# Attention's 256- and 128-column prompt products split into three products of high and low halves, with the scores one step later

## The chip, the cores and the metric

The kernel runs on one core of a Trainium2 chip. The metric is the device time of one execution in microseconds (us), the median of a few runs. TensorE (PE) multiplies; its weight loads are shown apart as PEld. VectorE (DVE) and ScalarE (ACT) do the elementwise work, GpSimd (POOL) a few small things and some transfers, and SyncE (SP) issues nearly all transfers, one after the other in one queue. Each engine takes its instructions strictly in the order written for it.

## The reference

One layer of a streaming encoder for two groups that share the weights: 256 prompt frames and 64 sample frames, 2048 features each. What matters here is the attention, eight heads of 128 features. For the prompt it is, per block of 128 queries and per head:

```python
z = jnp.einsum('bqhd,bkhd->bhqk', q_blk, k) * (SB_HEAD_DIM ** -0.5)
mask = k_pos[None, :] < q_pos[:, None]
log_beta = jax.nn.log_sigmoid(z)
log_stay = jnp.where(mask, jax.nn.log_sigmoid(-z), 0.0)
log_rest = lax.cumsum(log_stay, axis=3, reverse=True) - log_stay
w = jnp.where(mask, jnp.exp(log_beta + log_rest), 0.0)
o = jnp.einsum('bhqk,bkhd->bqhd', w, v)
```

Around it stand one wide input projection (q, k, v, a gating branch, merge gates), two branch projections, an output projection and a gated feed-forward net of 5632 features, with RMS norms between. All is float32.

## The kernel before

**Tiling.** Features lie on the 128 partitions, the 320 frames (256 prompt, 64 sample) on the free axis. A large projection is computed as blocks of 128 output features. Every float32 operand is split into a high half, rounded to the float32r format, and a low half, the rest. A product then is three float32r products: high x high, high x low, low x high (`product`, lines 83 to 85), each with 128 x 128 weights and 320 columns.

**Weight steps.** `block` walks over its input features in steps of eight blocks. A step loads 512 KB of weights (`raw`, line 70, three buffers), makes the high half `wh` on ACT (line 75) and the low half `wl` on DVE (line 76), four buffers each, and issues 24 products on PE. After each step `tick()` runs what was registered with `at` for that tick. I number the steps from 1, starting behind the opening phase (lines 183 to 280), which works off the first two heads in an order of its own. Step n's `raw` needs the buffer that the `wl` of step n-3 has read; step n's `wh` needs the buffer that PE has read in step n-4.

**Attention.** Heads go in four pairs, 0 to 3. For a pair `attend` registers, counted from the tick at which its q, k and v are there: `att_scores` (2 later), the transpose `att_turn` of v (6), the join of v (8), the load of cached v rows `att_rows` (11), `att_turn` of the weights w (12), their join (14) and `att_out` (16). `att_scores` has the score products on PE (lines 361, 362, 364), masking on DVE (368 to 371), three activations on ACT (376 to 378), suffix sums on DVE (386), a difference on DVE (389), exponentials on ACT (390 to 393) and a split of each float32 into two 16-bit planes (`apart`, 334). `att_turn` transposes the planes by a DMA from SP's queue (339), `att_join` puts them together on DVE (`together`, 344). `att_out` multiplies w with v (421), and ACT and DVE split the result into halves (117 and 118, 435 and 436). Score and output products are plain float32 here; the profile shows two PE rows for each.

**Order.** The kernel's text gives the work its sequence, but the framework lays out the order of each engine (and which of the rotating buffers is used) by a list scheduler of its own, within the data's dependencies; only the opening phase and what is marked with `keep_in_program_order` is fixed. So the order on DVE, ACT and SP has to be read from the built program, as below. PSUM has three `acc` buffers for the projections, four `aux` for attention, and a single `aux1`, which `att_out` and the norm `rms` (line 151) share. The tag `B` has 32 buffers for split activations of 320 columns.

Of the kernel before, what the change touches and what calls it, by code (L numbers as in the profile page):

```python
# [8 lines left out]
F32 = mybir.dt.float32  # L9
F32R = mybir.dt.float32r  # L10
AF = mybir.ActivationFunctionType
ALU = mybir.AluOpType

P = 128
TP = 256
# [18 lines left out]
def stream_step(ctx: ExitStack, tc: tile.TileContext, xT, w_in, w_a, w_b, w_out, w_gu, w_down,  # L34
                gains, ws_t, bs, ck_t, cv, y_t, k_t, v_t, sv_t):
    nc = tc.nc
# [21 lines left out]
    def at(tick, fn, *a):  # L58
        assert tick > state["tick"], (tick, state["tick"])
        later.setdefault(tick, []).append((fn, a))  # L60
# [38 lines left out]
    def slot(tag):  # L99
        return big.tile([P, T], F32R, tag=tag, bufs=32, name=tag)  # L100
# [182 lines left out]
    attn = {}  # L283
# [23 lines left out]
    Z, KT = 384, T + PAST  # L307
# [35 lines left out]
    def together(to, src):  # L343
        nc.vector.tensor_copy(to.bitcast(U16).rearrange("p (n w) -> p w n", w=2), src)
# [6 lines left out]
    def att_rows(p):  # L351
        cvt = attn[p]["cv"] = apool.tile([P, 2, 2, P], F32, tag="cv", name="cv")
        tc.keep_in_program_order(nc.sync.dma_start(out=cvt.rearrange("p i h d -> p i (h d)"),
                                                   in_=cv[:, :, 2 * p * P : (2 * p + 2) * P]))

    def att_scores(p):
        s = attn[p]
        q, k = s["q"], s["k"]
        za, zs = (aux(), aux()), aux()
        for j in range(2):  # L360
            nc.tensor.matmul(za[j][:, 0:P], q[:, j, 0:P], k[:, j, 0:P], start=True, stop=True)  # L361
            nc.tensor.matmul(za[j][:, P:Z], q[:, j, P:TP], k[:, j, 0:TP], start=True, stop=True)  # L362
        for j, r in enumerate(ROWS):
            nc.tensor.matmul(zs[r, 0 : KT - TP], q[:, j, TP:T], k[:, j, TP:KT], start=True, stop=True)  # L364
        z = s["z"] = pair("z0"), pair("z1")[:, 0 : Z + TS]
        for j in range(2):
            diag = [t[:, 0:Z].rearrange("p (i t) -> p i t", i=3)[:, 0:3:2, :] for t in (z[j], za[j])]
            nc.vector.tensor_tensor(out=diag[0], in0=diag[1], in1=mdiag.unsqueeze(1).broadcast_to([P, 2, P]), op=ALU.add)
            nc.vector.tensor_copy(z[j][:, P : 2 * P], za[j][:, P : 2 * P])
        nc.vector.tensor_tensor(out=z[1][:, Z:], in0=zs[:, 0:TS], in1=mown, op=ALU.add)  # L370
        nc.vector.tensor_copy(z[0][:, Z:], zs[:, TS : TS + PAST])

        es = []
        for zz in z:
            e = pair("e")[:, : zz.shape[1]]
            nc.scalar.activation(out=e, in_=zz, func=AF.Abs)
            nc.scalar.activation(out=e, in_=e, func=AF.Exp, scale=-1.0)
            nc.scalar.activation(out=e, in_=e, func=AF.Ln, bias=1.0)
            nc.vector.scalar_tensor_tensor(out=e, in0=zz, scalar=0.0, in1=e, op0=ALU.max, op1=ALU.add)
            es.append(e)  # L380


        for j, lo, hi, begin in ((0, 0, P, 0.0), (0, P, Z, 0.0), (1, 0, P, 0.0), (1, P, Z, 0.0),
                                 (1, Z, Z + TS, 0.0), (0, Z, Z + PAST, es[1][:, Z : Z + 1])):
            back = es[j][:, lo:hi][:, ::-1]
            nc.vector.tensor_tensor_scan(out=back, data0=ones[:, 0:1].broadcast_to([P, hi - lo]), data1=back,
                                         initial=begin, op0=ALU.mult, op1=ALU.add)
        for zz, e in zip(z, es):
            nc.vector.tensor_tensor(out=zz, in0=zz, in1=e, op=ALU.subtract)
        nc.scalar.activation(out=z[0], in_=z[0], func=AF.Exp)  # L390
        nc.scalar.activation(out=z[1][:, 0:Z], in_=z[1][:, 0:Z], func=AF.Exp)
        for r in ROWS:
            nc.scalar.activation(out=wown[r, r], in_=z[1][r, Z:], func=AF.Exp)

        y = s["wp"] = planes("wp0", 5 * P), planes("wp1", 4 * P)
        apart(y[0], z[0])
        apart(y[1][:, :, 0:Z], z[1][:, 0:Z])
        apart(y[1][:, :, Z:], wown)
# [7 lines left out]
    def att_join(p, what):  # L406
        s = attn[p]
        t = s[what]
        if what == "vt":
            av = s["av"] = apool.tile([P, 5 * P], F32, tag="av", name="av")  # L410
            together(av, t[0])
        else:
            wt = s["wt"] = apool.tile([P, 9 * P], F32, tag="wt", name="wt")
            together(wt[:, 0 : 5 * P], t[0])
            together(wt[:, 5 * P :], t[1])

    def att_out(p):
        s = attn.pop(p)
        wt, av, cvt = s["wt"], s["av"], s["cv"]
# [6 lines left out]
                lo = Z + i * P + j * TS  # L426
                mm(po[0][:, TP + j * TS : TP + (j + 1) * TS], cvt[:, i, j, :], wt[:, lo : lo + TS], False, i == 1)
        for j in range(2):
            w = wt[:, j * 5 * P : j * 5 * P + Z]
            mm(po[j][:, 0:TP], av[:, 2 * j * P : (2 * j + 1) * P], w[:, 0:TP], True, False)  # L430
            mm(po[j][:, P:TP], av[:, (2 * j + 1) * P : (2 * j + 2) * P], w[:, TP:], False, True)
        aT[2 * p] = split("B", po[0][:, 0:T])
        hi, lo = aT[2 * p + 1] = slot("B"), slot("B")
        for r, src in ((slice(0, TP), po[1][:, 0:TP]), (slice(TP, T), po[0][:, T : T + TS])):
# [24 lines left out]
                head_out(name, first[b][h][:, :T], h)  # L459

    def attend(p, now):
        at(now + 2, att_scores, p)
        at(now + 6, att_turn, p, "vt")
        at(now + 11, att_rows, p)
        at(now + 8, att_join, p, "vt")
        at(now + 12, att_turn, p, "wt")
        at(now + 14, att_join, p, "wt")
        at(now + 16, att_out, p)

    att_new(0)  # L470
    at(state["tick"] + 1, first_out)
# [248 lines left out]
```

## Time and profile before

| | us |
|---|---|
| median of 3 runs | 1709.8 (1708.69 to 1710.63) |
| profiled execution | 1708.48 |
| its span, first to last instruction | 1706.7 |
| PE busy | 1693.9 (99%) |
| DVE busy | 870.2 (51%) |
| ACT busy | 670.0 (39%) |
| POOL busy | 42.2 (2%) |

The granted TensorE clock is 0.997 over the span. Matmuls overlap in the rows, so what one costs in a stream is the distance from its start to the next one's start, not its own duration. Attention's work lies between about 48 and 255 us of the span; the rest is projections.

### The profile page before, as it was taken

The page shows a single profiled execution, that of the slowest core. Times are in us where ns is not written, and L with a number is a line of the kernel's source. Part 1 is how long each engine was busy: PE and PEld are TensorE (multiplying, and loading weights), DVE is VectorE, ACT ScalarE, POOL GpSimd, SP SyncE. Part 2 cuts the span into 40 slices and gives each one's busy share as a digit, 9 for nine tenths or more (in the row PEclk, how much of TensorE's full clock was granted, in tenths as well). Part 3 has the DMA queues.
Part 4 walks back from the last instruction along what each step waited for, and adds up shares of the span by engine and source line. Part 5 has one row for each costly group of instructions (what it writes and reads, how often), then busy time and mean ns, then how long its engine had stood idle before and what let it go on. Part 6 is the DMA issues. An engine that isn't in the chain of part 4 may idle for free.

```text
span 1706.7 us, 27337 instructions
## 1 busy us (share of the span) xinstructions
PE 1693.9 (99%) x11540; PEld 1688.5 (99%) x11540; DVE 870.2 (51%) x1105; ACT 670.0 (39%) x838; POOL 42.2 (2%) x65
## 2 busy tenths in 40 slices
PE   9999999999999999999999999999999999999997
PEld 9999999999999999999999999999999999999997
DVE  7665557544444445555444444444444444444455
ACT  6655555433333333443333332333333333333342
POOL 0000011000000000110000000000000000000000
PEclk9999999999999999999999999999999999999998
DMA  7575566544444445554444444444444444444453
GB/s 254 158 224 172 170 187 166 155 149 149 148 148 150 151 157 168 174 164 148 148 149 149 150 150 153 151 149 149 148 149 149 151 152 152 149 149 148 132 151 113
DMA packets 100299, 268.30 MB, mean 157 GB/s; under 512 B 28976, under 2 KB 35376, under 8 KB 100176
## 3 DMA queue, kind: packets, MB, share of 16 engines
q1 hardware_dynamic: 98672, 263.23, 48.7%
q0 software_dynamic: 1088, 3.02, 0.5%
q8 instruction: 90, 1.47, 0.3%
q10 hardware_dynamic: 416, 0.31, 0.1%
q14 instruction: 33, 0.27, 0.0%
HBM read 256.03 MB, written 5.51 MB: 153 GB/s over the span
## 4 chain that ended last, share of the span: by engine, by line
issue 54%; PE 44%; DVE 0%; DMA 0%; ACT 0%; POOL 0%; POOLq 0%; ACTq 0%; DVEq 0%
PE acc L83 14%; PE acc L84 13%; PE acc L85 13%; PE aux L219 2%; PE acc L219 1%; PE aux L421 1%; DVE h L659 0%; DMA raw<-w_in 0%; PE aux L530 0%; PE aux L362 0%; PE aux L364 0%; PE aux L361 0%; POOL sq_h L175 0%; PE aux L155 0%; PE aux L657 0%
## 5 line engine op out<-in xcount | busy, mean ns | idle before, releaser
L75 ACT CAST wh<-raw 128x1024 fp32r<-128x1024 f32 x468 | 484.2, 1036 | 962.8 <-PE acc L84 748.9
L76 DVE TENSOR_TENSOR wl<-raw,wh 128x1024 fp32r<-128x1024 f32 x468 | 564.6, 1207 | 477.9 <-ACT wh L75 477.1
L83 PE MATMUL acc<-A,wh 128*128 128x320 f32 x2464 | 762.9, 310 | 0.0
L84 PE MATMUL acc<-A,wh 128*128 128x320 f32 x2464 | 761.4, 309 | 0.0
L85 PE MATMUL acc<-A,wl 128*128 128x320 f32 x2464 | 761.4, 309 | 0.0
L83 PEld LDWEIGHTS acc<-A,wh 128*128 128x128 f32 x2464 | 462.6, 188 | 2.1 <-issue 2.0
L84 PEld LDWEIGHTS acc<-A,wh 128*128 128x128 f32 x2464 | 462.6, 188 | 0.2
L85 PEld LDWEIGHTS acc<-A,wl 128*128 128x128 f32 x2464 | 462.6, 188 | 0.0
L85 PE MATMUL acc<-B,wl 128*128 128x320 f32 x960 | 296.6, 309 | 0.0
L83 PE MATMUL acc<-B,wh 128*128 128x320 f32 x960 | 296.6, 309 | 0.0
L84 PE MATMUL acc<-B,wh 128*128 128x320 f32 x960 | 296.6, 309 | 0.0
L83 PEld LDWEIGHTS acc<-B,wh 128*128 128x128 f32 x960 | 180.2, 188 | 0.0
L84 PEld LDWEIGHTS acc<-B,wh 128*128 128x128 f32 x960 | 180.2, 188 | 0.0
L85 PEld LDWEIGHTS acc<-B,wl 128*128 128x128 f32 x960 | 180.2, 188 | 0.0
L83 PE MATMUL acc<-mh,wh 128*128 128x320 f32 x256 | 79.1, 309 | 0.0
L84 PE MATMUL acc<-ml,wh 128*128 128x320 f32 x256 | 79.1, 309 | 0.0
L85 PE MATMUL acc<-mh,wl 128*128 128x320 f32 x256 | 79.1, 309 | 0.0
L619 DVE TENSOR_TENSOR bb<-acc,rh 128x320 f32<-128x320 f32 x44 | 21.6, 492 | 57.8 <-PE acc L85 57.8
L616 DVE TENSOR_TENSOR ev<-acc,rh 128x320 f32<-128x320 f32 x44 | 21.6, 492 | 56.6 <-PE acc L85 56.6
L83 PEld LDWEIGHTS acc<-mh,wh 128*128 128x128 f32 x256 | 48.0, 188 | 0.0
L84 PEld LDWEIGHTS acc<-ml,wh 128*128 128x128 f32 x256 | 48.0, 188 | 0.0
L85 PEld LDWEIGHTS acc<-mh,wl 128*128 128x128 f32 x256 | 48.0, 188 | 0.0
(158 smaller groups left out, 691.9 us busy)
## 6 DMA issues: line engine op xcount, KB each, us to landing
raw<-w_gu SPq DMA_DIRECT2D x176, 512.0 KB, 3.6
raw<-w_in SPq DMA_DIRECT2D x141, 512.0 KB, 3.8
raw<-w_down SPq DMA_DIRECT2D x80, 512.0 KB, 3.5
raw<-w_out SPq DMA_DIRECT2D x32, 512.0 KB, 3.6
raw<-w_a SPq DMA_DIRECT2D x16, 512.0 KB, 3.5
raw<-w_b SPq DMA_DIRECT2D x16, 512.0 KB, 3.5
raw<-w_down SPq DMA_DIRECT2D x16, 256.0 KB, 2.6
xr<-xT SPq DMA_DIRECT2D x16, 160.0 KB, 2.6
```

Of the source, the lines that this page charges most:

```text
L75: nc.scalar.copy(out=wh[:, : n * P], in_=raw[:, : n * P])
L76: nc.vector.tensor_tensor(out=wl[:, : n * P], in0=raw[:, : n * P], in1=wh[:, : n * P].bitcast(F32), op=ALU.subtract)
L83: nc.tensor.matmul(ps[:, :T], a, x[0], start=first, stop=False)
L84: nc.tensor.matmul(ps[:, :T], a, x[1], start=False, stop=False)
L85: nc.tensor.matmul(ps[:, :T], b, x[0], start=False, stop=last)
L219: nc.tensor.matmul(first[b][h][:, :T], w[:, (h * n + j) * P : (h * n + j + 1) * P], xs[c + j][i], start=not last and c + j + i == 0, stop= ...
L421: mm = lambda out, a, b, first, last: nc.tensor.matmul(out, a, b, start=first, stop=last, skip_group_check=True)
L616: nc.vector.tensor_tensor(out=t, in0=pg, in1=got["rh"], op=ALU.mult)
L619: nc.vector.tensor_tensor(out=u, in0=pu, in1=got["rh"], op=ALU.mult)
```

## The change

`parts` splits a tile on the fly: the high half on ACT, the low half on DVE, each into a buffer of tag `B`. The prompt's queries, keys, v rows and weights w are split that way, ten splits per pair (eight of 256 columns, two of 128). Each prompt product of the scores and of the outputs becomes three float32r products. The sample's products (64 columns, and the 320-column product with 64 weight columns) stay as they are. `att_parts` runs one tick ahead of where the scores stood, and `att_scores`, `att_rows`, the turn and join of w and `att_out` come one tick later; the turn and join of v keep their ticks. The diff:

```diff
+    def parts(src):
+
+        n = src.free_size()
+        hi, lo = (slot("B")[:, 0:n] for _ in range(2))
+        view = lambda t: t.rearrange("p (j d) -> p j d", j=src.shape[1]) if len(src.shape) == 3 else t
+        nc.scalar.copy(out=view(hi), in_=src)
+        nc.vector.tensor_tensor(out=view(lo), in0=src, in1=view(hi.bitcast(F32)), op=ALU.subtract)
+        return hi, lo
+
+
+    THREE = ((0, 0), (0, 1), (1, 0))
+
+    def att_parts(p):
+        s = attn[p]
+        s["qp"] = parts(s["q"][:, :, P:TP])
+        s["q0"] = parts(s["q"][:, :, 0:P])
+        s["kp"] = [parts(s["k"][:, j, 0:TP]) for j in range(2)]
+
     def att_scores(p):
         s = attn[p]
-        q, k = s["q"], s["k"]
+        q, k, qp = s["q"], s["k"], s["qp"]
         za, zs = (aux(), aux()), aux()
         for j in range(2):
-            nc.tensor.matmul(za[j][:, 0:P], q[:, j, 0:P], k[:, j, 0:P], start=True, stop=True)
-            nc.tensor.matmul(za[j][:, P:Z], q[:, j, P:TP], k[:, j, 0:TP], start=True, stop=True)
+            for a, b in THREE:
+                nc.tensor.matmul(za[j][:, 0:P], s["q0"][a][:, j * P : (j + 1) * P], s["kp"][j][b][:, 0:P],
+                                 start=a + b == 0, stop=a == 1)
+            for a, b in THREE:
+                nc.tensor.matmul(za[j][:, P:Z], qp[a][:, j * P : (j + 1) * P], s["kp"][j][b], start=a + b == 0, stop=a == 1)
...
         if what == "vt":
             av = s["av"] = apool.tile([P, 5 * P], F32, tag="av", name="av")
             together(av, t[0])
+            s["ap"] = parts(av[:, 0 : 4 * P].rearrange("p (j d) -> p j d", j=2)[:, :, 0:P])
+            s["a1"] = parts(av[:, 0 : 4 * P].rearrange("p (j d) -> p j d", j=2)[:, :, P : 2 * P])
         else:
             wt = s["wt"] = apool.tile([P, 9 * P], F32, tag="wt", name="wt")
             together(wt[:, 0 : 5 * P], t[0])
             together(wt[:, 5 * P :], t[1])
+            s["tp"] = [parts(wt[:, j * 5 * P : j * 5 * P + TP]) for j in range(2)]
+            s["t1"] = [parts(wt[:, j * 5 * P + TP : j * 5 * P + Z]) for j in range(2)]
...
         for j in range(2):
-            w = wt[:, j * 5 * P : j * 5 * P + Z]
-            mm(po[j][:, 0:TP], av[:, 2 * j * P : (2 * j + 1) * P], w[:, 0:TP], True, False)
-            mm(po[j][:, P:TP], av[:, (2 * j + 1) * P : (2 * j + 2) * P], w[:, TP:], False, True)
+            for a, b in THREE:
+                mm(po[j][:, 0:TP], s["ap"][a][:, j * P : (j + 1) * P], s["tp"][j][b], a + b == 0, False)
+            for a, b in THREE:
+                mm(po[j][:, P:TP], s["a1"][a][:, j * P : (j + 1) * P], s["t1"][j][b], False, a == 1)
...
     def attend(p, now):
-        at(now + 2, att_scores, p)
+        at(now + 1, att_parts, p)
+        at(now + 3, att_scores, p)
         at(now + 6, att_turn, p, "vt")
-        at(now + 11, att_rows, p)
+        at(now + 12, att_rows, p)
         at(now + 8, att_join, p, "vt")
-        at(now + 12, att_turn, p, "wt")
-        at(now + 14, att_join, p, "wt")
-        at(now + 16, att_out, p)
+        at(now + 13, att_turn, p, "wt")
+        at(now + 15, att_join, p, "wt")
+        at(now + 17, att_out, p)
```

On PE the scores of pairs 0 to 3 stood ahead of steps 5, 15, 27 and 39, and stand now ahead of steps 6, 16, 28 and 40; `att_out` stood ahead of steps 19, 29, 41 and 53 and stands ahead of 20, 30, 42 and 54. The norm of the gating branch (the product of `sq_v` at line 155, into `aux1`) stood one whole step of 24 products behind the last `att_out`; now four products lie between them.

**Pair 1, the joins of w on DVE.** Names: `wl_n` is a step's low half, `av` and `wt` the joined v and w, `turned` what the transposes brought. Before, the row of `wl_1479` is step 23 and that of `wl_1512` is step 24:

```order
L76 TENSOR_TENSOR wl_1447<-raw_1444,wh_1446 128x1024
L118 TENSOR_TENSOR B_1332<-aux1_1320,B_1331 128x320
L436 TENSOR_TENSOR B_1336<-aux_1321,B_1335 128x256
L436 TENSOR_TENSOR B_1336<-aux1_1320,B_1335 128x64
L344 COPY av_1409<-turned_1341 128x2x640
L76 TENSOR_TENSOR wl_1479<-raw_1476,wh_1478 128x1024
L344 COPY wt_1611<-turned_1539 128x2x640
L344 COPY wt_1611<-turned_1541 128x2x512
L447 TENSOR_TENSOR k_1074<-acc_1348,rx_571 128x320
L76 TENSOR_TENSOR wl_1512<-raw_1509,wh_1511 128x1024
```

Now, from `wl_1567` (step 23) to `wl_1598` (step 24):

```order
L76 TENSOR_TENSOR wl_1567<-raw_1564,wh_1566 128x1024
L118 TENSOR_TENSOR B_1450<-aux1_1430,B_1449 128x320
L344 COPY av_1489<-turned_1392 128x2x640
L462 TENSOR_TENSOR B_1454<-aux_1431,B_1453 128x256
L462 TENSOR_TENSOR B_1454<-aux1_1430,B_1453 128x64
L362 TENSOR_TENSOR B_1492<-av_1489,B_1491 128x256
L362 TENSOR_TENSOR B_1496<-av_1489,B_1495 128x256
L344 COPY wt_1748<-turned_1665 128x2x640
L344 COPY wt_1748<-turned_1667 128x2x512
L473 TENSOR_TENSOR k_1106<-acc_1399,rx_571 128x320
L76 TENSOR_TENSOR wl_1598<-raw_1595,wh_1597 128x1024
```

The low half of step 24 stands behind the joins of w as it did, while the scores that these joins go back to stand one step later; and step 23's has moved ahead of the join of v.

**Pair 3, the join of v on DVE and its turn on SP.** Before, DVE has from the last difference on (`wl_2288`, `wl_2318` and `wl_2357` are steps 43, 44 and 45):

```order
L389 TENSOR_TENSOR z0_2088<-z0_2088,e_2096 128x640
L118 TENSOR_TENSOR B_2200<-aux1_2188,B_2199 128x320
L436 TENSOR_TENSOR B_2204<-aux_2189,B_2203 128x256
L76 TENSOR_TENSOR wl_2288<-raw_2285,wh_2287 128x1024
L436 TENSOR_TENSOR B_2204<-aux1_2188,B_2203 128x64
L76 TENSOR_TENSOR wl_2318<-raw_2315,wh_2317 128x1024
L344 COPY av_2345<-turned_2276 128x2x640
L491 TENSOR_TENSOR ev_2278<-acc_2215,rx_571 128x320
L76 TENSOR_TENSOR wl_2357<-raw_2354,wh_2356 128x1024
```

and now (`wl_2510` is step 44, `wl_2557` step 45; step 43's stands ahead of the whole chain of the scores):

```order
L410 TENSOR_TENSOR z0_2307<-z0_2307,e_2315 128x640
L118 TENSOR_TENSOR B_2429<-aux1_2409,B_2428 128x320
L76 TENSOR_TENSOR wl_2510<-raw_2507,wh_2509 128x1024
L518 TENSOR_TENSOR ev_2470<-acc_2378,rx_571 128x320
L462 TENSOR_TENSOR B_2433<-aux_2410,B_2432 128x256
L462 TENSOR_TENSOR B_2433<-aux1_2409,B_2432 128x64
L344 COPY av_2537<-turned_2468 128x2x640
L76 TENSOR_TENSOR wl_2557<-raw_2554,wh_2556 128x1024
```

The low half of step 45 stays behind the join of v. On SP the turn stood behind the 46th transfer of weights and stands now behind the 47th, whose buffer is free when step 44's low half is done.

**Pair 3, the exponentials on ACT.** `vs` is the first work of the gating branch, a GELU. Before:

```order
L376 ACTIVATE e_2096<-z0_2088 128x640
L376 ACTIVATE e_2101<-z1_2089 128x448
L377 ACTIVATE e_2096<-e_2096 128x640
L377 ACTIVATE e_2101<-e_2101 128x448
L378 ACT_TABLE_LOAD
L378 ACTIVATE e_2096<-e_2096 128x640
L378 ACTIVATE e_2101<-e_2101 128x448
L75 CAST wh_2287<-raw_2285 128x1024
```

and now:

```order
L519 ACT_TABLE_LOAD
L519 ACTIVATE vs_2151<-ev_2236 128x320
L171 ACTIVATE sq_v_2150<-vs_2151 128x320
L75 CAST wh_2479<-raw_2477 128x1024
L397 ACTIVATE e_2315<-z0_2307 128x640
L397 ACTIVATE e_2320<-z1_2308 128x448
L398 ACT_TABLE_LOAD
L398 ACTIVATE e_2315<-e_2315 128x640
L398 ACTIVATE e_2320<-e_2320 128x448
L399 ACT_TABLE_LOAD
L399 ACTIVATE e_2315<-e_2315 128x640
L399 ACTIVATE e_2320<-e_2320 128x448
```

A GELU has come ahead of pair 3's activations, and with it a table load ahead of line 398.

## Prediction

> **What bounds the kernel.** I read the page's busy times first, then the list of waits.
>
> ```profile
> PE 1693.9 (99%) x11540; PEld 1688.5 (99%) x11540; DVE 870.2 (51%) x1105; ACT 670.0 (39%) x838; POOL 42.2 (2%) x65
> PEld acc L83 <- issue: 2.0, 4, 0.5
> ACT wh L75 <- PE acc L84: 748.9, 339, 3.5
> ```
>
> PE is busy for 99% of the span, and the longest wait in front of its weight loads sums to 2.0 us. ACT waits 748.9 us for PE to give a weight buffer back: it runs ahead of PE by the four buffers. So PE's order is the whole time, and an edit costs what it adds to PE's own stream plus what it makes PE wait. The 51% and 39% of the helpers are averages; in the attention part they must be read place by place.
>
> **The products.** The timeline of PE around pair 0's scores:
>
> ```profile
> 62.54 0.31 PE L84 MATMUL acc<-A,wh 128*128 128x320 f32 x1
> 62.69 0.31 PE L85 MATMUL acc<-A,wl 128*128 128x320 f32 x1
> 62.84 0.38 PE L361 MATMUL aux<-k,q 128*128 128x128 f32 x2
> 63.06 0.60 PE L362 MATMUL aux<-k,q 128*128 128x256 f32 x2
> 63.49 0.39 PE L361 MATMUL aux<-k,q 128*128 128x128 f32 x2
> 63.71 0.60 PE L362 MATMUL aux<-k,q 128*128 128x256 f32 x2
> 64.24 0.76 PE L364 MATMUL aux<-k,q 128*64 128x320 f32 x4
> 64.93 0.41 PE L83 MATMUL acc<-A,wh 128*128 128x320 f32 x1
> ```
>
> From start to start a float32r product of 320 columns takes 0.147 (62.54 to 62.69 to 62.84; 24 of them, a step, 3.52). A float32 product is two rows: 0.22 for 128 columns (62.84 to 63.06), 0.43 for 256 (63.06 to 63.49), so one head's two take 0.65. The change turns each into three. No float32r product of 256 or 128 columns is in this trace. At the rate of the 320-column ones they take 0.147 x 256/320 = 0.117 and 0.059. But narrow products meet another limit, seen in pair 0's outputs:
>
> ```profile
> 116.73 1.00 PE L421 MATMUL aux<-wt,cv 128*128 128x64 f32 x8
> 117.57 1.53 PE L421 MATMUL aux<-wt,av 128*128 128x256 f32 x8
> ```
>
> Eight rows of 64 columns need 0.84, or 0.105 each, as long as a row of 128 columns (0.22/2 = 0.11), though they stream half as much: with 128 new weight columns each, a row does not go below about 0.11. I take 0.11 for 128 columns and 0.117 for 256: 3 x 0.227 = 0.68 per head in place of 0.65. There are 16 such heads (four pairs, two heads, scores and outputs): 16 x 0.03 = +0.5 us. Lower end, with no such limit: 3 x (0.059 + 0.117) = 0.53, 16 x -0.12 = -2.0. Upper end, a 128-column product at the whole float32 price: 3 x (0.22 + 0.117) = 1.01, 16 x 0.36 = +5.8. I take the 0.11 because the 64-column rows are nearest: same weights, narrow stream. The Trainium skill, page "TensorE: Matmul & The Clock Gate", section "Back-to-back issue gap", states about 81 ns per product of 128 columns in a stream of weight loads and products. By that figure the term would be an estimated 16 x (3 x (0.081 + 0.117) - 0.65) = -0.9; the rows here show 0.105 to 0.11, for float32.
>
> **The splits.** Ten casts on ACT and ten subtractions on DVE per pair, most of 256 columns:
>
> ```profile
> L209 ACT CAST wh<-raw 128x256 fp32r<-128x256 f32 x2 | 0.8, 398 | 1.2 <-DMA raw<-w_in 1.2
> L210 DVE TENSOR_TENSOR wl<-raw,wh 128x256 fp32r<-128x256 f32 x2 | 0.8, 422 | 1.0 <-ACT wh L209 1.0
> L75 ACT CAST wh<-raw 128x1024 fp32r<-128x1024 f32 x452 | 474.3, 1050 | 947.9 <-PE acc L84 734.0 <-issue 164.7 <-DMA raw<-w_in 42.1
> ```
>
> At most 10 x 0.40 = 4.0 on ACT and 4.2 on DVE per pair. I cost those of q and k at nothing: they run ahead of the scores, when ACT is waiting for a buffer. Those of v and w stand beside the joins, where DVE waits for transposes anyway. If that cover is gone, they add directly to the slips below.
>
> **Who is late next.** PE is fed by `wl`, which DVE makes in order, between attention's work. I compare, in the trace, when a low half ends and when PE needs it (the first L85 of that step). Pair 0, step 9, behind the whole chain of the scores:
>
> ```profile
> 77.92 3.49 DVE L76 TENSOR_TENSOR wl<-raw,wh 128x1024 fp32r<-128x1024 f32 x3
> 79.41 0.31 PE L85 MATMUL acc<-A,wl 128*128 128x320 f32 x1
> ```
>
> The first of the three ends at 77.92 + 1.23 = 79.1, needed at 79.4 (four steps behind 64.93): 0.3 to spare. Here the change moves chain and need together, from step 9 to step 10, and the low half goes ahead of the last scan and the two differences; I see no stall. In pairs 1 to 3 it does not move them together. The first low half behind the joins keeps its number (24, 36, 45), while the scores, and with them the joins, start a step, 3.52, later. Pair 1, step 24:
>
> ```profile
> 122.01 6.21 SPq L339 DMA_TRANSPOSE turned<-wp  x2
> 129.43 0.90 DVE L344 COPY wt<-turned 128x1280 uint16<-128x1280 uint16 x1 [2.24 <-DMA turned<-wp]
> 131.82 0.76 DVE L344 COPY wt<-turned 128x1024 uint16<-128x1024 uint16 x1 [1.48 <-DMA turned<-wp]
> 132.47 0.47 DVE L447 TENSOR_TENSOR k<-acc,rx 128x320 f32<-128x320 f32 x1
> 132.87 2.46 DVE L76 TENSOR_TENSOR wl<-raw,wh 128x1024 fp32r<-128x1024 f32 x2
> 136.82 0.31 PE L85 MATMUL acc<-A,wl 128*128 128x320 f32 x1
> ```
>
> Ready at 132.87 + 1.23 = 134.1, needed at 136.8: 2.7 to spare, less 3.5 is 0.8 late. To the chain come one low half ahead of the last scan (1.23) and a high half ahead of the planes' copies on ACT (1.05, the mean of its row): up to 3.1 late. Part of it hides, because the turn already waited in SP's queue behind a weight transfer. I take 2.0. Moved past on SP are also the turn and the load of cached rows; both come a step later with the step that needs them. Pair 2, step 36:
>
> ```profile
> 176.11 1.54 DVE L344 COPY wt<-turned 128x1280 uint16<-128x1280 uint16 x2 [2.57 <-DMA turned<-wp]
> 177.94 2.58 DVE L76 TENSOR_TENSOR wl<-raw,wh 128x1024 fp32r<-128x1024 f32 x2
> 183.69 0.31 PE L85 MATMUL acc<-A,wl 128*128 128x320 f32 x1
> ```
>
> Ready at 179.2, needed at 183.7: 4.5, less 3.5 is 1.0 to spare, less up to 2.3 again: 0 to 1.3 late; I take 0.3. Pair 3, step 45, behind the join of v:
>
> ```profile
> 199.90 1.28 ACT L378 ACT_TABLE_LOAD   x1
> 207.54 0.48 DVE L118 TENSOR_TENSOR B<-aux,B 128x320 fp32r<-128x320 f32 x1
> 208.62 1.22 DVE L76 TENSOR_TENSOR wl<-raw,wh 128x1024 fp32r<-128x1024 f32 x1
> 210.28 1.26 SPq L339 DMA_TRANSPOSE turned<-vp  x1
> 215.40 0.91 DVE L344 COPY av<-turned 128x1280 uint16<-128x1280 uint16 x1 [4.29 <-DMA turned<-vp]
> 216.19 0.48 DVE L491 TENSOR_TENSOR ev<-acc,rx 128x320 f32<-128x320 f32 x1
> 216.59 4.17 DVE L76 TENSOR_TENSOR wl<-raw,wh 128x1024 fp32r<-128x1024 f32 x3
> 219.99 0.31 PE L85 MATMUL acc<-A,wl 128*128 128x320 f32 x1
> ```
>
> Before, step 43's low half (208.62 to 209.84) frees a weight buffer, SP issues the transfer that waited for it and then the turn (210.28), the turn lands at 215.4, and step 45's low half ends at 216.59 + 1.22 = 217.8: 2.2 to spare. After, line 118 ends at 208.02 + 3.52 + 1.28 (the new table load, ahead of the exponential) - 0.4 (a DVE row, L491, that now stands earlier) = 212.4; step 44's low half follows, to 213.65; turn 214.1; landed 219.2 (5.12 as before); join and low half to 221.2 against 220.0: 1.2 late. The GELU brings two more table loads on ACT, 2.6 if they all count, so 1.2 to 3.8; I take 1.5. Last, the norm behind pair 3's outputs:
>
> ```profile
> 250.19 0.39 PE L83 MATMUL acc<-A,wh 128*128 128x320 f32 x1
> 250.88 0.56 DVE L436 TENSOR_TENSOR B<-aux,B 128x256 fp32r<-128x256 f32 x2
> ```
>
> `aux1` is free at 251.44, 1.25 behind the end of the outputs. The norm's product now comes four products, 0.59, behind them: 0 to 0.7 of waiting, I take 0.5.
>
> **Sum.** 0.5 (products) + 2.0 + 0.3 + 1.5 (low halves late) + 0.5 (norm) = +4.8. Against the profiled execution: 1708.48 (span 1706.7 and 1.8 around it) + 4.8 = 1713.3. The median shown is 1.3 above that execution: 1709.8 + 4.8 = 1714.6 us.
>
> **Rivals.** First, not slower: the cover holds. The slips stand or fall with the order on DVE. If the turns land as fast as 5.1 in pair 1 also (there the second join started 9.8 behind the issue), 2 or more of its slip go, and with pair 3 under its 2.2 only products and a bit of the norm are left, 0.5 to 1: 1710.5. For it: the list of waits shows ACT and DVE waiting most of the time. Against: that 3.52 is more than the 2.7 and 2.2 there are. It decides when the chains grow by less than the steps they lose.
>
> Second, the 128-column products cost the float32 price, +5.8 in place of +0.5: 1709.8 + 4.3 + 5.8 = 1719.9. For it: nothing here shows that the format keeps its rate when narrow. Against: the 64-column rows point to a floor of about 0.11, not 0.22.
>
> Third, they run at the streaming rate, -2.0: 1709.8 + 4.3 - 2.0 = 1712.1. For it: float32r at 320 columns never shows a weight-load limit. Against: the float32 rows do. The Trainium skill, same page, section "Weight-path perf modes", says that the fast weight load is on for 128 weights of any type but FP32; by that rule, if float32r counts as another type, the floor would not bind. No run here shows which.
>
> **Chances.** My forecast 0.50, with a range of its own from 1712 to 1718.5 (slips at 3 to 8); the cover holds 0.20; float32 price 0.20; streaming rate 0.10. A measurement tells a change from none at about 0.2%, 3.4 us here. Slower by more than that: 0.42 of the first, 0.20 of the second rival's, 0.01 of the third's, 0.63. Within it: 0.08 + 0.17 + 0.09 = 0.34. Faster: 0.03, out of the first rival, since even all products at the streaming rate give only -2.0. The range, 1709.5 to 1721, takes in the float32 price with the slips, and the cover with a small gain.
>
> **What would show it.** In the changed profile 48 rows each for the 128- and 256-column scores, spaced 0.11 and 0.117 (or 0.22: second rival; 0.06: third); DVE and ACT busier by at most 17 and 16 us; PE waiting for DVE's `wl` once for about 2 in pair 1 and once for 1.5 in pair 3, and for `aux1` at line 155 ahead of the norm. If PE shows no wait between 120 and 230 us, the first rival is right. A wait at pair 0, or PE waiting for the halves of q, k or w themselves, would mean that I misread the cover of the splits.

## The result, and the profile after

The changed kernel takes 1715.74 us (median of 6 runs, 1713.84 to 1716.58) against 1709.86 for the kernel before, run beside it (6 runs, 1708.59 to 1710.63): a ratio of 1.0033, with a 95% interval from 1.0023 to 1.0043, or +5.9 us. That is slower, by more than the 0.2% taken as the least that a measurement can tell. 1714.6 was forecast, and the range was 1709.5 to 1721.

The profiled execution took 1716.01, with a span of 1714.2. These are the page's busy times, and the whole list of what PE waited for (total us, times, longest us):

```profile
PE 1698.1 (99%) x11572; PEld 1693.7 (99%) x11572; DVE 883.4 (52%) x1145; ACT 684.7 (40%) x881; POOL 42.3 (2%) x65
```

```profile
PE acc L85 <- DVE wl L76: 2.6, 1, 2.6
PE acc L219 <- ACT wh L209: 1.5, 1, 1.5
PE aux L190 <- POOL ones L143: 1.2, 1, 1.2
PE aux L155 <- DVE B L462: 0.3, 1, 0.3
PE aux L684 <- POOL col L680: 0.2, 1, 0.2
```

Two of these are new. The wait at L85 for `wl` is the low half of a weight step that comes late; the one at L155 is the norm. DVE is busier by 13.2 and ACT by 14.7, a little under the 17 and 16 forecast as a ceiling. The products of pair 0's scores, in PE's timeline (start, length, and behind the x the number of rows grouped):

```profile
68.38 0.45 PE L380 MATMUL aux<-B 128*128 128x128 f32 x3
68.66 0.57 PE L383 MATMUL aux<-B 128*128 128x256 f32 x3
69.07 0.44 PE L380 MATMUL aux<-B 128*128 128x128 f32 x3
69.35 0.56 PE L383 MATMUL aux<-B 128*128 128x256 f32 x3
```

One head takes 69.07 - 68.38 = 0.69, against 0.65 before and 0.68 forecast. Row by row, the first narrow product is followed after 0.06, the other two after 0.11 each; the first wide one is followed after 0.17, the other two after 0.12. So the 0.28 and 0.41 of the groups mix two kinds of distance. (The list by form has 24 rows of each width for the scores and 24 for the outputs. The prediction's 48 are both together.) Pair 1, where 2.0 of stall had been forecast at step 24, in the queue of SP, on DVE and on PE:

```profile
128.05 6.63 SPq L339 DMA_TRANSPOSE turned<-wp  x2
135.76 1.62 DVE L344 COPY wt<-turned 128x1280 uint16<-128x1280 uint16 x2 [2.21 <-DMA turned<-wp]
137.28 0.47 DVE L473 TENSOR_TENSOR k<-acc,rx 128x320 f32<-128x320 f32 x1
137.67 2.35 DVE L76 TENSOR_TENSOR wl<-raw,wh 128x1024 fp32r<-128x1024 f32 x2
139.03 0.32 PE L85 MATMUL acc<-A,wl 128*128 128x320 f32 x1
```

The low half ends at about 138.9 and PE starts on it at 139.03, on time with some 0.15 left of the 2.7 there were. Pair 3, step 45, is where the time went. The chain from the scores' exponentials over the turn and the join of v to PE, rows of several engines in order of time:

```profile
204.95 1.28 ACT L398 ACT_TABLE_LOAD   x1
209.53 1.36 DVE L400 SCALAR_TENSOR_TENSOR e<-z,e 128x640 f32<-128x640 f32 x2 [3.25 <-ACT e L399]
213.21 1.14 POOL L175 TENSOR_TENSOR sq_v<-sq_v,sq 128x320 f32<-128x320 f32 x1 [20.27 <-ACT sq L174]
213.59 1.97 DVE L410 TENSOR_TENSOR z<-z,e 128x448 f32<-128x448 f32 x2
215.48 0.48 DVE L118 TENSOR_TENSOR B<-aux,B 128x320 fp32r<-128x320 f32 x1
215.88 1.21 DVE L76 TENSOR_TENSOR wl<-raw,wh 128x1024 fp32r<-128x1024 f32 x1
217.53 1.74 SPq L339 DMA_TRANSPOSE turned<-vp  x1
222.62 0.86 POOL L175 TENSOR_TENSOR sq_v<-sq_v,sq 128x320 f32<-128x320 f32 x1 [8.28 <-ACT sq L174]
222.65 1.57 DVE L344 COPY av<-turned 128x1280 uint16<-128x1280 uint16 x1 [2.72 <-DMA turned<-vp]
224.12 1.20 DVE L76 TENSOR_TENSOR wl<-raw,wh 128x1024 fp32r<-128x1024 f32 x1
225.37 0.63 PE L85 MATMUL acc<-A,wl 128*128 128x320 f32 x1 [2.58 <-DVE wl L76]
```

PE stands still for 2.6 us until step 45's low half is there. Something further follows, shown by a table of stretches around it (us, PE's busy time and instructions, then the granted clock):

```profile
220.00:225.00 5.00, 2.79 (x18) 1.00 0.47 93
225.00:229.00 4.00, 3.63 (x15) 0.57 0.60 174
```

Behind the wait the granted clock is down to 0.57 as a mean of four microseconds; by finer stretches it is 0.50 from 225.22 to 228.63. From 225.80 to 228.47 products of 320 columns start every 0.267 instead of 0.147. And the norm:

```profile
261.87 0.78 PE L155 MATMUL aux<-sq_v,ones 128*128 128x320 f32 x2 [0.31 <-DVE B L462]
```

To find where the difference arises, I read from the PE timelines of the profiled executions when the first products of steps 1, 20, 28, 44, 46 and 60 start, and set the lengths of the stretches against those of the kernel before. Behind step 60 none differs from the kernel before by more than 0.03. The opening phase, which no kernel here changes, is left out: it ends between 48.76 (the kernel before) and 51.15 in these executions, and 50.78 in that of the changed kernel, so that its span is 2.0 longer for a reason outside the change. (Its 320-column products start every 0.267 until 9.9 and every 0.147 from 10.2 on; in the kernel before they stand 0.147 apart as early as 5.8.)

| kernel, us against before | steps 1-19 (pair 0) | 20-27 (pair 1) | 28-43 (pair 2) | 44, 45 (join of v, pair 3) | 46-59 (pair 3, norm) | sum |
|---|---|---|---|---|---|---|
| changed kernel | +0.14 | +0.02 | +0.29 | +4.48 | +0.61 | +5.5 |
| delay alone | -0.08 | -0.02 | +0.10 | +4.41 | +0.07 | +4.5 |
| split products alone | +0.27 | +1.17 | +0.19 | 0.00 | +0.07 | +1.7 |
| own buffer for turned v | +0.14 | +0.52 | +0.29 | 0.00 | +0.61 | +1.6 |
| norm one tile later | +0.14 | +0.06 | +0.29 | +5.73 | +0.13 | +6.4 |
| 12 fillers | +0.14 | 0.00 | +0.29 | +2.97 | +0.62 | +4.0 |
| 6 fillers | +0.14 | +0.09 | +0.29 | +3.04 | +0.62 | +4.2 |
| 3 fillers | +0.14 | +0.14 | +0.29 | +4.45 | +0.61 | +5.6 |
| two additions left out | +0.14 | 0.00 | +0.29 | +1.77 | +0.62 | +2.8 |
| both cures | +0.14 | 0.00 | +0.29 | 0.00 | +0.07 | +0.5 |
| both cures, alternating | +0.07 | +0.13 | +0.28 | 0.00 | +0.08 | +0.6 |
| both cures, 256 only | -0.53 | -0.17 | -0.34 | +0.98 | -0.16 | -0.2 |

Of the +5.5 in the changed kernel, 4.5 lie in two weight steps of pair 3. The other rows are the experiments. Where they show a short wait with the clock at 1.00, the stretch grows by the wait and some 0.3 more: 0.25 of waiting cost 0.52, 0.70 cost 0.98, 0.84 cost 1.17 and 1.51 cost 1.77.

### The profile page after: what moved, and what is told of

Read it like the earlier page. It is cut to its first block, busy times and chain, and to the rows that moved or that the text cites. A ratio compares the mean times of both kernels' runs of the same rounds, so it can differ in the third digit from the quotient of the medians.

```text
span 1714.2 us, 27481 instructions
## 1 busy us (share of the span) xinstructions
PE 1698.1 (99%) x11572; PEld 1693.7 (99%) x11572; DVE 883.4 (52%) x1145; ACT 684.7 (40%) x881; POOL 42.3 (2%) x65
## 4 chain that ended last, share of the span: by engine, by line
issue 54%; PE 43%; DVE 1%; ACT 1%; DMA 1%; POOL 0%; POOLq 0%; ACTq 0%; DVEq 0%; SPq 0%
PE acc L85 13%; PE acc L83 13%; PE acc L84 13%; PE aux L219 2%; PE acc L219 1%; PE aux L446 0%; DVE h L686 0%; DMA turned<-vp 0%; DMA raw<-w_in 0%; DVE wl L76 0%; PE aux L557 0%; DVE e L407 0%; PE aux L383 0%; PE aux L385 0%; DVE z L410 0%
## 5 line engine op out<-in xcount | busy, mean ns | idle before, releaser
L85 PE MATMUL acc<-A,wl 128*128 128x320 f32 x2464 | 762.2, 309 | 2.6 <-DVE wl L76 2.6
L85 PEld LDWEIGHTS acc<-A,wl 128*128 128x128 f32 x2464 | 463.1, 188 | 2.9 <-DVE wl L76 2.8
L85 PE MATMUL acc<-B,wl 128*128 128x320 f32 x960 | 296.6, 309 | 0.0
L85 PEld LDWEIGHTS acc<-B,wl 128*128 128x128 f32 x960 | 180.2, 188 | 0.0
L85 PE MATMUL acc<-mh,wl 128*128 128x320 f32 x256 | 79.1, 309 | 0.0
L85 PEld LDWEIGHTS acc<-mh,wl 128*128 128x128 f32 x256 | 48.1, 188 | 0.0
```

What stands on the lines that cost most here:

```text
L85: nc.tensor.matmul(ps[:, :T], b, x[0], start=False, stop=last)
```

## Experiments

### The delay alone

The kernel before, float32 products and no splits, with the ticks of the change:

```diff
-        at(now + 2, att_scores, p)
+        at(now + 3, att_scores, p)
...
-        at(now + 11, att_rows, p)
+        at(now + 12, att_rows, p)
...
-        at(now + 12, att_turn, p, "wt")
-        at(now + 14, att_join, p, "wt")
-        at(now + 16, att_out, p)
+        at(now + 13, att_turn, p, "wt")
+        at(now + 15, att_join, p, "wt")
+        at(now + 17, att_out, p)
```

> The kernel before with only the times of the scores, the load of cached rows, the turn and join of w and the outputs moved one tile later; products stay float32, no splits. Theory (the delay costs, through the join of v in pair 3): without the products' +0.5 and with the norm's wait, about +5 us against before, 1714.8, with PE waiting 2 to 3 us at line 85 near 220 us for a low half of the weights, and the granted clock falling behind it. Rival A (the splits on ACT and DVE make the low half late) and rival B (the split products cost it): 1709.9, no such wait.

Measured: 1714.92 against 1710.29, ratio 1.0029 (1.0018 to 1.0040). From its list of waits, its DVE and POOL timelines and its stretches:

```profile
PE acc L85 <- DVE wl L76: 2.6, 1, 2.6
```

```profile
222.16 0.86 POOL L175 TENSOR_TENSOR sq_v<-sq_v,sq 128x320 f32<-128x320 f32 x1 [8.28 <-ACT sq L174]
222.17 1.59 DVE L344 COPY av<-turned 128x1280 uint16<-128x1280 uint16 x1 [2.71 <-DMA turned<-vp]
```

```profile
225.00:229.00 4.00, 4.00 (x18) 0.59 0.69 209
```

The same wait of 2.6, the same long join and the same fall of the clock, without one split product. So it is the delay that costs. What the theory had wrong is the norm: here it stands nine products behind the outputs instead of four, and PE's list shows no wait for it.

### The split products alone

The changed kernel with the ticks of before (the edit above in reverse; the splits stay at +1).

> The split products and their splits, with the times of the kernel before (splits at +1, scores at +2). Theory: only the products' +0.5 is left, 1710.4, up to 1711 if PE waits for the halves of q and k, which are now made right ahead of the scores; no wait near 220 us. Rivals A and B: about 1715, as after.

Measured: 1711.41 against 1710.29, ratio 1.0006 (0.9997 to 1.0015). No wait near 220 us. The time is 0.4 above the 1711 that the theory allowed, and PE's timeline has a wait that I had not expected:

```profile
136.21 0.42 PE L85 MATMUL acc<-A,wl 128*128 128x320 f32 x1 [0.84 <-DVE wl L76]
```

It is pair 1's, at step 23: the low half now stands behind both joins of w. The clock stays at 1.00. In the table this kernel's +1.7 is that wait's 1.17 and 0.5 of products. Rivals A and B (the splits' load on ACT and DVE, and the products) fall as the cause of the 4 to 5 us in pair 3.

### A buffer of its own for pair 3's turned v

Why does the turn wait for the scores at all, when v is there long before? In SP's order it stands behind ten weight transfers that follow pair 2's turns of w. In the built program its target is one of the eight buffers of tag `D`, the one that the second `e` of pair 3's scores occupies until line 410 (`turned_2468` and `e_2320` have the same address). The edit gives it another buffer:

```diff
-    def turn(src):
-        to = planes("turned", src.shape[2])
+    def turn(src, own=False):
+        to = (lambda t: t[:, 0 : src.shape[2]].bitcast(U16).rearrange("p (w n) -> p w n", w=2))(apool.tile([P, 2 * T], F32, tag="own", name="own") if own else pair("turned"))
...
-        s[what] = [turn(t) for t in ((s["vp"],) if what == "vt" else s["wp"])]
+        s[what] = [turn(t, what == "vt" and p == 3) for t in ((s["vp"],) if what == "vt" else s["wp"])]
```

> The changed kernel, with a buffer of its own for the turned v of pair 3 in place of one of the eight that it shares with the scores' tiles; the turn then stands five weight transfers earlier in SP's queue and the join ahead of the last scan. Theory: PE's 2.6 us wait at line 85 near 225 us goes, and with it the stretch at a lower clock: -4.4, 1711.3; if only the wait goes and the clock falls anyway, -2.7, 1713.0. Rival A (DVE is late because it has more to do): DVE has the same work, so at most -1, 1714.7.

Measured: 1711.54 against 1710.29, ratio 1.0009 (1.0001 to 1.0018). SP's and DVE's timelines:

```profile
191.95 1.76 SPq L339 DMA_TRANSPOSE own<-vp  x1
...
213.31 0.88 DVE L344 COPY av<-own 128x1280 uint16<-128x1280 uint16 x1
...
217.02 2.35 DVE L76 TENSOR_TENSOR wl<-raw,wh 128x1024 fp32r<-128x1024 f32 x2
```

The turn stands five transfers earlier and goes out 25.6 us earlier, and steps 44 and 45 together take what they took before, 7.04: the wait and the lower clock are gone together. DVE has the same work as in the changed kernel, so its load was not the cause. Against the kernel before, the medians are 1.3 apart instead of 5.9, and the traces 1.6 instead of 5.5. The 0.5 in pair 1 comes with a wait of 0.25 there in this execution, with an order that is the same up to that place, so pair 1 stands on the edge.

### The norm one tile later

The norm, and the gain of its first pair, come one tile later.

```diff
-    at(base + 1, sgu_norm)
+    at(base + 2, sgu_norm)
     for p, mix in enumerate((9, 11, 14, 18)):
-        at(base + 1 + 3 * p, sgu_gain, p)
+        at(base + (2, 4, 7, 10)[p], sgu_gain, p)
```

> The changed kernel with the norm of the spatial gate, and the gain of its first pair, one tile later. Theory: PE's wait for the bank of pair 3's outputs ahead of line 155 goes: -0.6 to -0.9 against after, about 1715.0; the wait near 225 us stays at 2.6. Rival (the wait there is hidden, or the norm one tile later makes the first mix late): 1715.7 or more.

Measured: 1715.01 against 1710.29, ratio 1.0030 (1.0019 to 1.0042). By the times alone this can't be told from the changed kernel (1.0033). The trace tells it: the wait at L155 is gone from the list, and steps 46 to 59 are +0.13 instead of +0.61, so the norm was worth 0.5. The stretches showed something else, with the same 2.6 us of waiting in pair 3:

```profile
220.40:223.81 3.41, 1.50 (x10) 1.00 0.31 67
223.81:227.22 3.41, 2.73 (x10) 0.50 0.49 115
227.22:230.63 3.41, 3.41 (x15) 0.50 0.94 324
```

Here the lower clock lasts 6.8 us instead of 3.4, and steps 44 and 45 cost +5.73 instead of +4.48. What differs is where the wait lies: it runs from 221.90 to 224.49, and the clock falls before it is over.

### Filling the wait: twelve, six and three products

Products of ones stand ahead of step 45's first product with `wl`. They write into free columns of the block's own bank with a start of their own, in the middle of the block's sum, and that block's result is then not the one of the changed kernel. The number of products is that of the run; here it is twelve.

```diff
-WARM = 7
+WARM, FILL = 7, 12
...
-        wh, wl = w
+        (wh, wl), state["n"] = w, state.get("n", 0) + 1
...
-        nc.tensor.matmul(ps[:, :T], b, x[0], start=False, stop=last)
+        [tc.keep_in_program_order(nc.tensor.matmul(ps[:, 384:512], ones, ones, start=True, stop=True, skip_group_check=True)) for _ in range(FILL * (state["n"] == 8 * 44 + 1))]; nc.tensor.matmul(ps[:, :T], b, x[0], start=False, stop=last)
```

> The changed kernel, in which twelve float32 products of 128 columns (0.22 each, 2.64 together), whose result nobody reads, stand ahead of line 85's first product of step 45, where PE waits 2.6 us. Theory (PE's idling sets the clock back): the wait is filled, the granted clock stays 1.00, and the low half still comes as late: -1.6 against after (11 products at 0.267 in place of 0.147 go, and 0.3 of the start), about 1714.1. Rival (the clock falls there for another reason, such as load on the chip): the clock still falls, 1715.7.

> As the one before with six products, 1.3 us, so that PE idles for the last 1.3 us of the wait. It tells how much idling sets the clock back. If the share of idle time in a stretch of some microseconds decides, 1.3 may be too little: clock 1.00, 1714.1. If any stop of a microsecond does it: the clock falls, 1715.7.

> As the twelve fillers with three, 0.66 us, so that PE idles for about 1.9 us. With 1.3 us idle the clock stayed at 1.00, with 2.6 it fell to 0.50. If the limit lies above 1.9: clock 1.00 and about 1714.3; if below: 0.50 for some 3 us and about 1715.7.

Measured: 1714.12 with twelve, ratio 1.0024 (1.0015 to 1.0032) against 1710.36; 1714.64 with six, 1.0027 (1.0016 to 1.0039); a single run with three, 1716.09. PE's waits there are none, 1.3 and 1.8. The stretches from 225 to 229 us, of the kernels with twelve, six and three:

```profile
225.00:229.00 4.00, 4.00 (x29) 1.00 0.91 313
```

```profile
225.00:229.00 4.00, 3.65 (x25) 1.00 0.62 166
```

```profile
225.00:229.00 4.00, 3.64 (x15) 0.59 0.59 160
```

Twelve fillers delay step 45 as before: its low half ends 6.6 to 6.7 us behind the start of step 44 in both kernels. (POOL's addition now holds up this low half, 1.88 instead of 1.20, and not the join, 0.89 instead of 1.57; the sum is the same.) But the clock stays up: steps 44 and 45 cost +2.97 instead of +4.48. So 1.5 of the changed kernel's time is the clock's answer to PE's idling. Here idling for 1.3 leaves it alone, and 1.8 brings it down.

### Without POOL's additions

In the changed kernel the differences at line 410 took 1.97, and the join of v 1.57 instead of 0.91; beside each stands an addition of POOL. In the kernel before, the two differences took 1.33:

```profile
206.29 1.33 DVE L389 TENSOR_TENSOR z<-z,e 128x448 f32<-128x448 f32 x2
```

This kernel leaves out those two additions, so that the norm's sum lacks the squares of two heads.

```diff
-            self.n = 0
+            self.n, self.v = 0, name == "sq_v"
...
-                (engine or nc.gpsimd).tensor_tensor(out=self.total, in0=self.total, in1=sq, op=ALU.add)
+                self.v and self.n in (1, 2) or (engine or nc.gpsimd).tensor_tensor(out=self.total, in0=self.total, in1=sq, op=ALU.add)
```

> The changed kernel without two of POOL's additions at line 175 (the squares of the gate's second and third head are left out of the norm's sum); nothing moves on the other engines. In the changed kernel the differences at line 410 took 1.97 while POOL added at 213.21 (before: 1.33), and the join of v 1.57 while it added at 222.62 (before: 0.91). Theory (DVE is held up by POOL's addition): these rows go back to 1.33 and 0.91, and PE's wait ahead of step 45's first product at line 85 from 2.6 to 1.3; after 1.3 us idle the clock stayed at 1.00 so far, so that 1.3 + 1.5 go: 1713.0. If the wait ends above 1.8, the clock falls and 1714.8 is the time. Rival (these rows are long for another reason, such as the transposes' traffic): both stay, 1715.7.

Measured: 1713.23 against 1710.39, ratio 1.0015 (1.0006 to 1.0024). DVE's timeline, PE's wait and the stretch:

```profile
213.21 1.33 DVE L410 TENSOR_TENSOR z<-z,e 128x448 f32<-128x448 f32 x2
...
221.69 0.89 DVE L344 COPY av<-turned 128x1280 uint16<-128x1280 uint16 x1 [2.65 <-DMA turned<-vp]
```

```profile
PE acc L85 <- DVE wl L76: 1.5, 1, 1.5
```

```profile
225.00:229.00 4.00, 4.00 (x30) 1.00 0.88 306
```

Both rows are back at their old length, the wait shrinks to 1.5, and at 1.5 the clock holds. Two additions of about 1 us on an engine that is busy for 2% of the span were worth 2.7 us in steps 44 and 45 (4.48 - 1.77): 1.1 of waiting, and with it the fall of the clock. The sign of it stands in the profile before: there three low halves from 216.59 on take 4.17 us, against 3.49 for the three from 77.92 on, and beside them POOL has an addition from 217.82 to 219.67.

### Both cures

The own buffer and the later norm together.

> The changed kernel with both cures: a buffer of its own for pair 3's turned v, and the norm one tile later. Theory: what is left is the products' +0.5 and up to 0.5 in pair 1, whose low half of step 24 came between 0.3 late and 0.15 early in the runs so far: 1710.6, not to be told from before. Rival (part of the cost lies elsewhere and the cures don't add): 1711.5 or more.

Measured: 1711.27 against 1710.36, ratio 1.0006 (0.9998 to 1.0015). Behind the opening phase its profiled execution is 0.50 longer than that of before, all of it in the stretches with products. PE's list of waits has nothing new against before. The time alone lies between the two expectations (1710.6 and 1711.5) and can't tell them apart; by the trace the cures add up.

### Both cures, wide and narrow products alternating

```diff
             for a, b in THREE:
+                nc.tensor.matmul(za[j][:, P:Z], qp[a][:, j * P : (j + 1) * P], s["kp"][j][b], start=a + b == 0, stop=a == 1, skip_group_check=True)
                 nc.tensor.matmul(za[j][:, 0:P], s["q0"][a][:, j * P : (j + 1) * P], s["kp"][j][b][:, 0:P],
-                                 start=a + b == 0, stop=a == 1)
-            for a, b in THREE:
-                nc.tensor.matmul(za[j][:, P:Z], qp[a][:, j * P : (j + 1) * P], s["kp"][j][b], start=a + b == 0, stop=a == 1)
+                                 start=a + b == 0, stop=a == 1, skip_group_check=True)
...
             for a, b in THREE:
                 mm(po[j][:, 0:TP], s["ap"][a][:, j * P : (j + 1) * P], s["tp"][j][b], a + b == 0, False)
-            for a, b in THREE:
                 mm(po[j][:, P:TP], s["a1"][a][:, j * P : (j + 1) * P], s["t1"][j][b], False, a == 1)
```

The narrow product's start falls into the open sum of the wide one in the same bank, and the prompt's result is then not the one of the changed kernel.

> The one before, with the products of 256 and of 128 columns alternating in place of three and three. Theory (a narrow product is bound by the load of its weights, about 0.1, which a wide product ahead of it covers): six loads of 0.1 per head, 0.60 against 0.69, 16 heads: -1.4, 1709.2, and the narrow ones spaced under 0.1. Rival A (a narrow product has a price of 0.11 of its own): no change, 1710.6. Rival B (with alternation all run at the streaming rate, 0.117 + 0.058): 0.53 per head, -2.6, 1708.0.

Measured: 1711.29 against 1710.36, ratio 1.0002 (0.9993 to 1.0011). PE's timeline:

```profile
68.93 0.34 PE L380 MATMUL aux<-B 128*128 128x256 f32 x1
69.11 0.23 PE L381 MATMUL aux<-B 128*128 128x128 f32 x1
69.17 0.33 PE L380 MATMUL aux<-B 128*128 128x256 f32 x1
69.33 0.22 PE L381 MATMUL aux<-B 128*128 128x128 f32 x1
```

A narrow product is followed after 0.06, a wide one after 0.17; together 0.23, as 0.11 + 0.117 in the order before. None of the three expectations holds whole: rival A gets the time right, but a narrow product has no price of its own of 0.11 (0.06 here). What fits is that each product needs a load of weights of about 0.115, and the theory's 0.1 was too low: 6 x 0.115 = 0.69, which three narrow and three wide products take in both orders once they follow each other. In PEld's rows the loads start 0.11 to 0.12 apart in both orders, however the products lie. That a wide product covers the load behind it, and that what a narrow one leaves uncovered is paid by the next, is my reading of these distances; no run changes the size of the weights.

### Both cures, only the 256-column products split

```diff
-        s["q0"] = parts(s["q"][:, :, 0:P])
...
-            for a, b in THREE:
-                nc.tensor.matmul(za[j][:, 0:P], s["q0"][a][:, j * P : (j + 1) * P], s["kp"][j][b][:, 0:P],
-                                 start=a + b == 0, stop=a == 1)
+            nc.tensor.matmul(za[j][:, 0:P], q[:, j, 0:P], k[:, j, 0:P], start=True, stop=True)
...
-            for a, b in THREE:
-                mm(po[j][:, P:TP], s["a1"][a][:, j * P : (j + 1) * P], s["t1"][j][b], False, a == 1)
+            mm(po[j][:, P:TP], av[:, (2 * j + 1) * P : (2 * j + 2) * P], wt[:, j * 5 * P + TP : j * 5 * P + Z], False, True)
```

(and without the splits `a1` and `t1`)

> The kernel with both cures, in which only the products of 256 columns are three of halves; those of 128 columns are float32 again and their splits gone. Theory (what costs is a row's load of weights, 0.11 to 0.117, so three rows beat two only where a float32 row takes 0.22 for 256 columns, not where it takes 0.11 for 128): 0.22 + 3 x 0.117 = 0.57 per head against 0.65 before and 0.69 with both split, 16 x -0.08 = -1.3 against before, 1709.0, at most 1710 if the first row behind a narrow one takes 0.17. Rival (the order that the scheduler now finds on ACT and DVE makes a low half late again): 1711 or more, with a wait at line 85.

Measured: 1710.08 against 1710.10, ratio 1.0000 (0.9991 to 1.0009). PE's timeline:

```profile
66.93 0.38 PE L379 MATMUL aux<-k,q 128*128 128x128 f32 x2
67.07 0.60 PE L383 MATMUL aux<-B 128*128 128x256 f32 x3
67.51 0.39 PE L379 MATMUL aux<-k,q 128*128 128x128 f32 x2
...
220.40 0.41 PE L85 MATMUL acc<-A,wl 128*128 128x320 f32 x1 [0.70 <-DVE wl L76]
```

A head takes 67.51 - 66.93 = 0.58, as the theory had it, and the three stretches ahead of pair 3's join are 1.0 shorter than before. The rival's case came true in its wait, though not in its time (1711 or more): a wait of 0.7 at step 45, +0.98 for steps 44 and 45, gives the gain back. So the forecast of 1709.0 was missed by as much. No version here beats the kernel before by more than can be measured.

## Why the prediction was right, and where its terms were off

The sum came out right (+4.8 forecast, +5.9 in the medians, +5.5 behind the opening phase in the traces), and so did its sign and the mechanism in pair 3. But two terms were wrong in opposite directions: pair 1 was 2.0 too high, and pair 3, with the clock behind it, 3.0 too low. That the sum came so close is luck. The forecast also had its largest part in pair 1, where nothing was lost.

- **Products, +0.5.** Right: 0.50 with both cures. The 0.11 for 128 columns, taken from the float32 rows of 64 columns, held for float32r. The second rival (0.22 each) and the third (0.06 each) are out; 0.06 stands only behind the first narrow product after a wide one. The Trainium skill, page "TensorE: Matmul & The Clock Gate", section "Back-to-back issue gap", would have given -0.9 with its 81 ns; the trace does not agree for this format. By the Trainium skill, same page, section "Weight-path perf modes", the fast weight load would be on if float32r counted as other than FP32; the 0.11 of the traces does not show it at work, for the float32 rows of 128 columns take 0.11 as well.
- **Splits at nothing.** Right: PE waited for none of the halves of q, k, v or w, and pair 0 had no wait.
- **Pair 1, +2.0.** Wrong, 0 in the changed kernel (0 to 0.5 with the same order in other executions). The step that failed is the sum that added the slip, and more, to a chain taken as fixed behind the turn. The chain was not fixed. Before, the second join of w started 9.8 behind the turn's issue; now the turn was issued at 128.05, and the two joins followed each other from 135.76, the second about 8.6 behind. That gave back 1.2. And the turn came only 3.8 us nearer to the need (14.8 ahead of it before, 11.0 now): the slip of 3.5 and 0.3 of the up to 2.3 that the longer chain could add. So of the 2.7 there were, 2.7 - 3.8 + 1.2 left a margin of 0.1. That is the direction of the first rival, though not its size: it had set the turns' landing at 5.1.
- **Pair 2, +0.3.** 0: PE's list has no wait there, and the +0.29 of steps 28 to 43 stays with both cures, as part of the products' 0.50.
- **Pair 3, +1.5.** The mechanism was the one forecast (SP's turn, join, low half, PE), but mis-sized: 2.6 of waiting, and +4.48 with what came behind it. The transpose took the 5.12 that were carried over (217.53 to 222.65). What was not seen are the two rows beside POOL's additions, 0.64 at line 410 and 0.66 at the join. Without them the wait was 1.5, the value I took (a choice between 1.2 and 3.8, so in part luck), and it cost 1.77. What I had down as the reason for the turn's place, SP's queue behind a weight transfer, was only its last link: the transfer order itself follows from the shared buffer.
- **The clock, no term.** 1.5 of the +4.48 came from the granted clock behind the wait. The sum charged a stall of PE at its own length.
- **Norm, +0.5.** Right: 0.48 between the two traces with the norm in either place (0.61 - 0.13). But it hangs on the place that the scheduler finds, four products behind the outputs here and nine with the delay alone.

The first rival, not slower, was right about pair 1 and needed pair 3 to stay under its 2.2 to spare as well; pair 3 went over.

## What to carry to other kernels

When a step is moved later, look for what it holds as well as for what it feeds: here the moved scores kept a buffer that a transfer of other data needed, and one buffer more gave back 3.9 of the 5.5 us in the traces. Price a new stall of TensorE as the stall plus what the clock does behind it, and look beside the chain for work on POOL. And three products of halves pay only where a float32 row streams longer than its weights load: at 256 columns (0.35 against 0.43), not at 128 (about 0.34 against 0.22).

## What the hardware showed

**The clock counts PE's idle time in fixed stretches of 3.41 us.** Within a trace the changes of the granted clock lie whole numbers of 3.413 us apart. In the changed kernel it rises at 10.18, falls at 225.22, which is 63 such stretches later, and rises at 228.63. It was low for one stretch in the changed kernel, with the delay alone and with three fillers, and for two with the later norm. Counting the stretches on from these changes, PE idled for 2.6, 2.4, 1.9 and 1.8 us of the one that ends at the fall (delay alone, changed kernel, later norm, three fillers). The clock held after 1.51 and 1.26 us in one stretch (two additions left out, six fillers). That the share of a stretch decides fits these cases, and so would the length of the wait. Two waits in the opening phase speak for the share:

```profile
4.30:7.71 3.41, 1.84 (x11) 1.00 1.02 314
7.71:11.12 3.41, 3.41 (x15) 0.50 1.01 351
4.75:8.16 3.41, 2.03 (x11) 1.00 0.99 308
8.16:11.00 2.84, 2.84 (x22) 1.00 1.03 360
```

The first two lines are the kernel with the own buffer, the others the one that splits only the 256-column products. In the first, a wait of 1.57 us lies in one stretch, and the clock falls. In the other, a wait of 1.61 has 1.38 in the stretch, and the clock holds. All these cases fit a limit between 1.51 and 1.57 us of idling, some 45% of a stretch; no run aimed at it. With the later norm 0.68 of the wait lies in the stretch behind the fall, and the clock stays low for one stretch more: the same 2.6 us of waiting cost +5.73 there and +4.48 in the changed kernel. The Trainium skill, page "TensorE: Matmul & The Clock Gate", section "Part 1: The HAM clock gate", says that half speed comes after at least one idle window of about 3.4 us, in windows that run freely. The stretches agree with the windows and their length; that a whole one must be idle does not, since 1.57 of 3.41 us was enough.

**POOL's additions hold up DVE.** Beside an addition of 0.9 to 1.1 us on POOL two DVE instructions with both operands in SBUF took 1.97 instead of 1.33, and a copy 1.57 instead of 0.91; without the addition they were back at 1.33 and 0.89. It matters which of the two starts first. In the changed kernel the addition starts at 222.62 and the join at 222.65, and the join is long. With twelve fillers the join starts at 220.82 and the addition at 220.84: the join takes its 0.89, the addition 1.56 instead of 0.86, and the low half that DVE has next 1.88 instead of 1.20. The Trainium skill, page "SBUF — State Buffer", section "SBUF: two separate sides", says that DVE and GpSimd share a pair of ports that one instruction holds to its end; the runs agree in that the first holds up the second (by 0.6 to 0.7 us here), and don't show the ports themselves.

**A float32r product with new 128 x 128 weights takes about 0.115 us, with 128 columns as with 256,** in either order, although the first narrow product behind a wide one is followed after 0.06. The load of the weights is the likely price: in PEld's rows the loads start 0.11 to 0.12 apart throughout. The Trainium skill, page "TensorE: Matmul & The Clock Gate", section "LDWEIGHTS (loading the stationary operand)", has columns / 1.2 in ns for a load, an estimated 107 ns for 128; the 0.11 to 0.12 of the rows is a little more.
